# Decay sums of a linear-attention layer: one head behind each projection, and a stacked split matmul for their low-rank product

## The chip, the cores and the metric

The kernel runs on one core of a Trainium2 chip. The metric is the device time of one execution in microseconds. The kernel before took 2865.96 us, the median of three runs (2865.26 to 2868.37).

## The reference, cut to what matters

One inference step of a two-layer model: 128 context tokens and 1024 latent tokens, 1024 features. The first layer normalizes and modulates its input, projects it, and runs windowed attention beside a gated linear attention (GLA) with 4 heads in two directions. The change touches the projections and the decay of the GLA:

```python
h = rmsnorm(x, g) * (1 + scale) + shift
qa, ka, va, qb, kb, vb, rb, lr = split_cols(h @ w_in, SIZES_EVEN)   # lr: 2 directions x rank 16
...
la = log_sigmoid(einsum('btzr,zrk->btzk', lr, w_alpha) + b_alpha) / 16
la = la.reshape(B, T, 2, B_HEADS, B_DK)                             # 4 heads of 64, forward and backward
...
bcum = cumsum(la in chunks of 64 tokens)                            # the decay sums of the GLA
```

Keys and queries of the attention are rotated (`rope_2d`) behind their projection. The rest (attention, GLA, output projection, feed-forward, a recurrent second layer) is left as it is.

## The kernel before, in words

Features lie on the 128 partitions, the 1152 tokens (context first) on the free axis, in three column blocks of 384. A projection (`proj`, lines 292 to 302) is, for each column block, 8 times three matmuls: weights and activations are each split into a high and a low part of type fp32r, and `mm3` (lines 147 to 150) multiplies high by high, high by low, low by high. A weight tile comes through `wload` (lines 129 to 141): a transfer, ACT's cast to the high part (139), GpSimd's subtraction for the low part (140).

Memory is handed out in numbered slots of 128 x 1152: `us(i)` (line 84) is a new tile in slot i, and the first write into it waits until the tile that had the slot before has been read for the last time. `us(32)` and `us(33)` are halves of one pair (`up`, line 79). A matmul's target is a PSUM bank, 3 of the kind "mm", 2 of "S", 2 of "X", 1 of "O"; a bank is free when what it held has been read. The program is written as one sequence; a scheduler with a timeline simulation (line 1429) then fixes the order on each engine ahead of time, from its own costs. On the chip every engine and the transfer queue of SP work through their order strictly, so an instruction that waits holds up all behind it.

**The first stretch.** The input X lies in slots 16 to 23. Each column block is normalized in turn (`norm`, 281; `norm_k`, 263): sums of squares, row sums on TensorE (229), square root and reciprocal (231, 232), a broadcast on TensorE (239) copied by ACT (260), then for each of the 8 rows k a product on GpSimd (267), scale and shift on ACT or VectorE (272, 273, 275, 277) and the low part on VectorE (278). Nine blocks of 128 tokens are multiplied by the values', gates' and low-rank weights (lines 615 to 617), two tiles a block, 24 matmuls a tile. ACT copies the first tile of a block out (620), VectorE the second (620); line 623 copies the last 32 columns of the second, the low-rank factors `lr`, into `lrs3`. The norms of the second and third column block are started at block 2 and 5. Then TensorE transposes the low-rank columns (630) into `lrt` (631).

**The second stretch.** `gla_pre(hd)` (641 to 655) makes the decay sums of one head: for each column block a matmul of the 32 low-rank rows, fp32 (647), and a bias on ACT (648) into `et`; then on all 1152 tokens VectorE (649), Exp (650) and Ln (651) on ACT, each with a load of its table, VectorE (652), two scans of VectorE over 64 partitions, forward (653) and backward (654), into `bt`, and a store (655). `et` and `bt` have one slot each, 31 and 30, so a head's bias waits for the scans of the head before. The four heads stand in a row (657). Behind them come, in the program: the projection of the keys KA and its rotation (`rope`, 664 to 670: a shuffle, a product, GpSimd's product 669, a sum), the projection of the values VST and its transposes (705), the stacked split of the keys (`kstack`, 708 to 718), four query projections (720 to 724), each with its rotation and a store to `d_qa`; then the attention, which reads `d_qa` back (738, 744) and begins on TensorE at line 776. The scheduler spreads this over time; projections of the GLA's own keys and queries fill TensorE between. Line 192 is a piece of the modulation of later layers, spread over the kernel.

Of the kernel before, what the change touches and what calls it, by code (L numbers as in the profile page):

```python
# [8 lines left out]
F32R = mybir.dt.float32r  # L9
# [3 lines left out]
ALU = mybir.AluOpType  # L13
# [5 lines left out]
CW = 384  # L19
# [4 lines left out]
U = T  # L24
# [22 lines left out]
def body(tc, A):  # L47
    nc = tc.nc
    ve, sc, pe, gp, sy = nc.vector, nc.scalar, nc.tensor, nc.gpsimd, nc.sync

    def f_(ap):
        return ap.bitcast(F32)

    with contextlib.ExitStack() as ctx:
# [24 lines left out]
        def up(i, dt=F32):  # L79

            pair[i] = pu.tile([128, 2 * U], dt, tag=f"u{i}", name=f"u{i}", bufs=1)
            return pair[i]

        def us(i, dt=F32):

            if i in (0, 32):
                return up(i, dt)[:, :U]
            if i in (1, 33):
                return pair[i - 1][:, U:]
            return pu.tile([128, U], dt, tag=f"u{i}", name=f"u{i}", bufs=1)  # L90
# [7 lines left out]
        def mmps():  # L98
            if wide[0]:
                wide[0] = wide[0] % 8 + 1  # L100
                if wide[0] > 3 and wide[0] <= wide[1]:
                    return aux(*(("X", 2), ("X", 2), ("S", 2), ("S", 2), ("O", 1))[wide[0] - 4])
                if wide[0] > wide[1]:
                    wide[0] = 1
            return pm.tile([128, 512], F32, name="mm", bufs=3)

        def tmpa(n=CW):
            t = pt.tile([128, CW], F32, name="ta", bufs=3)
            return t[:, :n]

        def aux(tag="S", bufs=2):
            return pm.tile([128, 512], F32, name=tag, bufs=bufs)
# [8 lines left out]
        def wtile():  # L121

            if wext:
                wpos[0] = (wpos[0] + 1) % (4 + len(wext))
                if wpos[0] >= 4:
                    i = wext[wpos[0] - 4]
                    return uc(i - 100, F32R) if i >= 100 else us(i, F32R)[:, :D]
            return pw.tile([128, D], F32R, name="w", bufs=4)
# [3 lines left out]
        def wload(ap, n=D, slots=None, he=None):  # L132
            raw = pw.tile([128, D], F32, name="raw", bufs=3)
            sy.dma_start(out=raw[:, :n], in_=ap)
            if slots:
                hi, lo = us(slots[0], F32R), us(slots[1], F32R)
            else:
                hi, lo = wtile(), wtile()
            (he or wcopy[0])(hi[:, :n], raw[:, :n])  # L139
            gp.tensor_tensor(out=lo[:, :n], in0=raw[:, :n], in1=f_(hi[:, :n]), op=ALU.subtract)  # L140
            return hi, lo

        def split(hi, lo, src, e=None):
            sc.copy(hi, src)
            return (e or ve).tensor_tensor(out=lo, in0=src, in1=f_(hi), op=ALU.subtract)  # L145
# [13 lines left out]
        def ch(c):  # L159
            return slice(c * CW, (c + 1) * CW)  # L160
# [11 lines left out]
        def load_x(c):  # L172
            for k in range(8):
                sy.dma_start(out=X[k][:, ch(c)], in_=A["xT"][k, :, ch(c)])
# [117 lines left out]
        def projc(w, H, evict, c):  # L292
            hi, lo = w
            ps = mmps()
            for k in range(8):
                s = slice(k * 128, (k + 1) * 128)
                mm3(ps[:, :CW], hi[:, s], lo[:, s], H[0][k][:, ch(c)], H[1][k][:, ch(c)], k == 0, k == 7)
            evict(c, ps[:, :CW])

        def proj(w, H, evict):  # L300
            for c in range(NCH):
                projc(w, H, evict, c)
# [259 lines left out]
        d_qa = dr.tile([4, 128, T], F32, name="d_qa")  # L562
# [22 lines left out]
        H = [[None] * 8, [None] * 8]  # L585
# [15 lines left out]
                    sc.copy(wh[:, s], raw)  # L601
                    (gp if hf == 0 or i else ve).tensor_tensor(out=wl[:, s], in0=raw, in1=f_(wh[:, s]), op=ALU.subtract)
        load_x(2)
        lrs3 = us(32)[:, :288].rearrange("p (b n) -> p b n", b=9)
        for blk in range(9):
            if blk in (2, 5):
                norm(0, 0, X, H, 1 if blk == 2 else 2, inplace=True)
# [1 line left out]
            for hf in range(2):  # L609
                ps = mmps()  # L610
# [7 lines left out]
                n = 272 if hf == 0 else 240  # L618
# [3 lines left out]
                if hf == 1:  # L622
                    ve.tensor_copy(lrs3[:, blk], ps[:, 240:272])

        lrt = us(33)[0:32]
        for b0, b1 in ((0, 4), (4, 8), (8, 9)):
            ps = aux()
            n = (b1 - b0) * 128
            for b in range(b0, b1):
                pe.transpose(ps[0:32, (b - b0) * 128:(b - b0 + 1) * 128], lrs3[:, b], ident)  # L630
            ve.tensor_copy(lrt[:, b0 * 128:b1 * 128], ps[0:32, :n])

        RM = us(23)
        gp.memset(RM, 1.0)
        rm = RM.rearrange("p (c t) -> p c t", t=64)
        gp.memset(rm[0:64, :, 0:1], 0.0)
        gp.memset(rm[64:128, :, 63:64], 0.0)
        walp = us(22)[0:32, :512].rearrange("p (h n) -> p h n", h=4)
        sy.dma_start(out=walp, in_=A["w_alp"])

        def gla_pre(hd):

            et, bt = us(31), us(30)
            bal = cols[:, C_BALPHA + hd:C_BALPHA + hd + 1]
            for c in range(NCH):
                ps = aux()
                pe.matmul(ps[:, :CW], walp[:, hd], lrt[:, ch(c)], start=True, stop=True)
                sc.activation(out=et[:, ch(c)], in_=ps[:, :CW], func=AF.Identity, bias=bal)
            ve.scalar_tensor_tensor(bt, et, -1.0, et, op0=ALU.mult, op1=ALU.min)
            sc.activation(out=bt, in_=bt, func=AF.Exp)  # L650
            sc.activation(out=bt, in_=bt, func=AF.Ln, bias=1.0)
            ve.scalar_tensor_tensor(et, et, 0.0, bt, op0=ALU.min, op1=ALU.subtract)
            ve.tensor_tensor_scan(bt[0:64], RM[0:64], et[0:64], 0.0, op0=ALU.mult, op1=ALU.add)
            ve.tensor_tensor_scan(bt[64:128, ::-1], RM[64:128, ::-1], et[64:128, ::-1], 0.0, op0=ALU.mult, op1=ALU.add)
            sy.dma_start(out=d_b[hd], in_=bt)

        for hd in range(4):
            gla_pre(hd)

        COS, SIN = us(16), us(17)  # L660
        sy.dma_start(out=COS[:, :TL], in_=A["rope"][0])
# [2 lines left out]
        def rope(t):  # L664
            x = t[:, TC:T]
            r = us(19)[:, :TL]
            ve.stream_shuffle(r, x, [(i + 16) % 32 for i in range(32)])
            ve.tensor_tensor(out=x, in0=x, in1=COS[:, :TL], op=ALU.mult)
            gp.tensor_tensor(out=r, in0=r, in1=SIN[:, :TL], op=ALU.mult)
            ve.tensor_tensor(out=x, in0=x, in1=r, op=ALU.add)  # L670

        def ev_to(t):
            def ev(c, ps):
                sc.copy(t[:, ch(c)], ps)
            return ev

        KA, VST = us(18), us(20)
        proj(wload(A["w_ef"][4]), H, ev_to(KA))
        sy.dma_start(out=A["o_ck"], in_=KA[:, :TC])
        rope(KA)  # L680
        proj(wload(A["w_ef"][5]), H, ev_to(VST))
# [1 line left out]

        KK = [[us(24 + g * 2 + part, F32R) for part in range(2)] for g in range(2)]
        VA = [us(28, F32R), us(29, F32R)]
        SM = us(30, F32R)
        cst = tmpa(256)
        sy.dma_start(out=cst[:, 0:128], in_=A["cache_v"])
        sy.dma_start(out=cst[:, 128:256], in_=A["cache_k"])
        split(SM[:, 0:128], SM[:, 128:256], cst[:, 0:128])  # L690

        def va(part, blk):
            if blk == 9:
                return SM[:, part * 128:part * 128 + 128]
            return VA[part][:, blk * 128:(blk + 1) * 128]

        def kkc(g, part):
            o = 256 + (g * 2 + part) * 128
            return SM[:, o:o + 128]

        for b0, b1 in ((0, 4), (4, 8), (8, 9)):
            ps = aux()
            n = (b1 - b0) * 128
            for b in range(b0, b1):
                pe.transpose(ps[:, (b - b0) * 128:(b - b0 + 1) * 128], VST[:, b * 128:(b + 1) * 128], ident)
            split(VA[0][:, b0 * 128:b1 * 128], VA[1][:, b0 * 128:b1 * 128], ps[:, :n])

# [9 lines left out]
            kstack(cst[:, 128:256], KK[g][0][:, TL:U], KK[g][1][:, TL:U], g)  # L717
            kstack(KA[:, 0:TC], kkc(g, 0), kkc(g, 1), g)

        for j in range(4):  # L720
            q = us(21 + j % 2)
            proj(wload(A["w_ef"][j]), H, ev_to(q))
            rope(q)
            sy.dma_start(out=d_qa[j], in_=q)

# [530 lines left out]
        for blk in range(3):  # L1256
# [3 lines left out]
            g = gates_a(blk, 1)  # L1260
# [172 lines left out]
```

## Time and profile before

| | before |
|---|---|
| median of 3 runs | 2865.96 us (2865.26 to 2868.37) |
| profiled execution | 2866.14 us, span 2864.4 us |
| mean granted TensorE clock | 0.96 |
| TensorE busy | 2671.9 us, 93% |
| VectorE busy | 2036.7 us, 71% |
| ACT busy | 1333.5 us, 47% |
| GpSimd busy | 1280.0 us, 45% |
| chain that ended last | TensorE 73%, VectorE 12%, ACT 5%, transfers 5% |

PE is TensorE's matmul queue, DVE is VectorE, POOL is GpSimd, SP the queue of transfers. The span runs from the first to the last instruction; 1.7 us of the execution's own time lie around it. Busy time is the mean over a program of many stages, so a change in one stage is read in that stage's own rows.

### The profile page before, as it was taken

Reading aid. Unit: us, or ns where it says so; the run is one execution under the profiler, and the core shown is the slowest. Engines: PE = TensorE matmul, PEld = TensorE weight load, DVE = VectorE, ACT = ScalarE, POOL = GpSimd, SP = SyncE. Lnnn points to the kernel's source line nnn. Section 1 sums busy time; section 2 is a strip of 40 time slices with the busy share of each in tenths; the row PEclk is TensorE's granted clock in tenths of the full one; section 3 lists DMA queues with packets and bytes.
Section 4 is the critical chain, followed back from the end, with each engine's and each line's share of the span. In section 5 each row is a group of like instructions: output and inputs, shape, how many; then the busy total and the mean of one; then the engine's idle time right before and its main releaser. Section 6 shows DMA issues by size and latency. Waiting matters only on the chain.

```text
span 2864.4 us, 48327 instructions
## 1 busy us (share of the span) xinstructions
PE 2671.9 (93%) x18588; PEld 2540.8 (89%) x18588; DVE 2036.7 (71%) x3536; ACT 1333.5 (47%) x2402; POOL 1280.0 (45%) x767
## 2 busy tenths in 40 slices
PE   6999996888899999999999989896899999999998
PEld 4888884556899999999999989896899999999998
DVE  5466677653688877778786566657788777788876
ACT  5445556434543434444335567563543533444333
POOL 4231014223555556455556433333555555455453
PEclk8999997889999999999999999898999999999999
DMA  7125347643342233523223133373342233433322
GB/s 280 58 94 170 127 151 235 198 138 123 109 174 87 84 101 101 202 85 101 82 86 121 61 104 101 110 238 131 129 158 82 89 96 119 162 92 107 101 82 71
DMA packets 136966, 353.64 MB, mean 123 GB/s; under 512 B 14592, under 2 KB 61824, under 8 KB 136736
## 3 DMA queue, kind: packets, MB, share of 16 engines
q1 hardware_dynamic: 135008, 343.48, 36.3%
q0 software_dynamic: 1728, 7.08, 0.7%
q8 instruction: 146, 2.39, 0.3%
q14 instruction: 84, 0.69, 0.1%
HBM read 286.20 MB, written 64.30 MB: 122 GB/s over the span
## 4 chain that ended last, share of the span: by engine, by line
PE 73%; DVE 12%; ACT 5%; DMA 5%; issue 3%; POOL 1%; SPq 0%; DVEq 0%; ACTq 0%; POOLq 0%
PE mm L150 10%; PE mm L148 10%; PE mm L149 10%; PE X L150 5%; PE X L148 5%; PE X L149 5%; PE S L148 4%; PE S L150 4%; PE S L149 4%; PE O L148 2%; PE O L150 2%; PE O L149 2%; PE mm L192 1%; PE X L814 1%; DVE u L943 1%
## 5 line engine op out<-in xcount | busy, mean ns | idle before, releaser
L150 PE MATMUL mm<-u,w 128*128 128x384 f32 (+1 forms) x1320 | 420.9, 321 | 2.4 <-DVE w L458 2.0
L148 PE MATMUL mm<-u,w 128*128 128x288 f32 (+1 forms) x1234 | 396.6, 322 | 25.0 <-DVE u L317 23.1
L149 PE MATMUL mm<-u,w 128*128 128x288 f32 (+1 forms) x1234 | 393.4, 319 | 3.2 <-POOL u L145 3.2
L140 POOL TENSOR_TENSOR w<-raw,w 128x1024 fp32r<-128x1024 f32 (+1 forms) x66 | 150.3, 2278 | 361.3 <-ACT w L139 306.8
L148 PEld LDWEIGHTS mm<-u,w 128*128 128x128 f32 x1234 | 235.5, 191 | 33.8 <-issue 27.9
L150 PEld LDWEIGHTS mm<-u,w 128*128 128x128 f32 x1320 | 251.0, 190 | 7.5 <-issue 4.3
L149 PEld LDWEIGHTS mm<-u,w 128*128 128x128 f32 x1234 | 235.2, 191 | 4.6 <-POOL u L145 3.4
L150 PE MATMUL mm<-u,u 128*128 128x288 f32 x693 | 204.0, 296 | 0.0
L148 PE MATMUL S<-u,w 128*128 128x288 f32 (+1 forms) x526 | 164.9, 314 | 38.9 <-ACT t L1177 33.5
L317 DVE SCALAR_TENSOR_TENSOR u<-mm,mods,u 128x288 f32<-128x288 f32 (+4 forms) x345 | 145.8, 451 | 74.4 <-PE mm L150 73.7
L150 PE MATMUL X<-u,w 128*128 128x288 f32 (+1 forms) x630 | 192.8, 307 | 1.6 <-DVE w L450 1.6
L148 PE MATMUL mm<-u,u 128*128 128x288 f32 x627 | 186.5, 298 | 4.0 <-ACT u L444 3.8
L149 PE MATMUL mm<-u,u 128*128 128x288 f32 x627 | 185.3, 296 | 0.0
L148 PE MATMUL X<-u,w 128*128 128x288 f32 (+1 forms) x580 | 176.2, 306 | 1.4 <-DVE u L145 1.2
L149 PE MATMUL X<-u,w 128*128 128x288 f32 (+1 forms) x580 | 176.3, 305 | 1.1 <-DVE u L278 1.1
L149 PE MATMUL S<-u,w 128*128 128x288 f32 (+1 forms) x526 | 163.5, 311 | 0.0
L148 PE MATMUL mm<-u,c 128*128 128x288 f32 (+2 forms) x497 | 152.4, 307 | 0.7 <-DVE ta L505 0.7
L451 POOL TENSOR_TENSOR u<-raw 128x512 f32<-128x512 f32 x82 | 136.0, 1658 | 35.2 <-DMA raw<-in_w_fi_dram 19.4
L149 PE MATMUL mm<-u,c 128*128 128x288 f32 (+2 forms) x497 | 151.4, 305 | 0.0
L447 DVE TENSOR_TENSOR u<-u,raw 128x512 f32<-128x512 f32 x82 | 140.3, 1711 | 0.8
L148 PEld LDWEIGHTS S<-u,w 128*128 128x128 f32 x526 | 101.7, 193 | 41.8 <-ACT t L1177 35.6
L148 PE MATMUL X<-u,u 128*128 128x288 f32 (+1 forms) x444 | 131.9, 297 | 2.2 <-DVE u L145 1.5
(443 smaller groups left out, 9114.9 us busy)
## 6 DMA issues: line engine op xcount, KB each, us to landing
raw<-in_w_fi_dram SPq DMA_DIRECT2D x164, 512.0 KB, 3.6
raw<-in_w_fo_dram SPq DMA_DIRECT2D x96, 384.0 KB, 3.1
raw<-in_w_ada_dram SPq DMA_DIRECT2D x48, 512.0 KB, 4.9
c<-in_w_ada_dram SPq DMA_DIRECT2D x32, 512.0 KB, 5.9
d_w<-u SPq DMA_DIRECT2D x20, 512.0 KB, 4.0
u<-d_w SPq DMA_DIRECT2D x20, 512.0 KB, 4.8
u<-in_w_ada_dram SPq DMA_DIRECT2D x16, 512.0 KB, 10.3
raw<-in_w_fo_dram SPq DMA_DIRECT2D x16, 512.0 KB, 3.7
```

The costliest lines, as they stand in the source:

```text
L140: gp.tensor_tensor(out=lo[:, :n], in0=raw[:, :n], in1=f_(hi[:, :n]), op=ALU.subtract)
L148: pe.matmul(ps, wh, hh, start=first, stop=False)
L149: pe.matmul(ps, wh, hl, start=False, stop=False)
L150: pe.matmul(ps, wl, hh, start=False, stop=last)
L192: pe.matmul(ps[32 * g:32 * g + 32, :256], scp[:, 4 * p + g], raw[:, g * 256:(g + 1) * 256], start=p == 0, stop=p == 1)
L317: ve.scalar_tensor_tensor(x, ps[:, s0:s1], mod(l, j, cond, n), x, op0=ALU.mult, op1=ALU.add)
L447: ve.tensor_tensor(out=s2, in0=s1, in1=a11, op=ALU.subtract)
L451: gp.tensor_tensor(out=s3, in0=a11, in1=a21, op=ALU.subtract)
L814: pe.transpose(px[:, i * 128:(i + 1) * 128], P[i][:, kb * 128:(kb + 1) * 128], ident)
L943: ve.tensor_tensor_scan(kv[Bk, ::-1], D0[Bk, ::-1], kv[Bk, ::-1], 0.0, op0=ALU.mult, op1=ALU.add)
```

## The change

The decay sums of a head move: head 0 stands behind the projection of the keys, heads 1 and 2 behind the first two query projections, head 3 behind the third. The transposed low-rank factors and their weights are split into high and low parts and stacked on 96 partitions (high, high, low against high, low, high), so that one fp32r matmul of 96 rows takes the place of the fp32 one of 32 rows. The pair slot 32/33 now holds that stack, so `lrs3` moves to slot 21, which is X[5], and `w_alp` is loaded into slot 20, which is X[4].

```diff
@@ -601,7 +601,7 @@
                     sc.copy(wh[:, s], raw)
                     (gp if hf == 0 or i else ve).tensor_tensor(out=wl[:, s], in0=raw, in1=f_(wh[:, s]), op=ALU.subtract)
         load_x(2)
-        lrs3 = us(32)[:, :288].rearrange("p (b n) -> p b n", b=9)
+        lrs3 = us(21)[:, :288].rearrange("p (b n) -> p b n", b=9)
         for blk in range(9):
             if blk in (2, 5):
                 norm(0, 0, X, H, 1 if blk == 2 else 2, inplace=True)
@@ -622,21 +622,29 @@
                 if hf == 1:
                     ve.tensor_copy(lrs3[:, blk], ps[:, 240:272])
 
-        lrt = us(33)[0:32]
+        lw = up(32, F32R)
+        lrt = lw[:, :U]
         for b0, b1 in ((0, 4), (4, 8), (8, 9)):
             ps = aux()
             n = (b1 - b0) * 128
             for b in range(b0, b1):
                 pe.transpose(ps[0:32, (b - b0) * 128:(b - b0 + 1) * 128], lrs3[:, b], ident)
-            ve.tensor_copy(lrt[:, b0 * 128:b1 * 128], ps[0:32, :n])
+            g = slice(b0 * 128, b1 * 128)
+            for q in range(2):
+                sc.copy(lrt[q * 32:q * 32 + 32, g], ps[0:32, :n])
+            ve.tensor_tensor(out=lrt[64:96, g], in0=ps[0:32, :n], in1=f_(lrt[0:32, g]), op=ALU.subtract)
 
         RM = us(23)
         gp.memset(RM, 1.0)
         rm = RM.rearrange("p (c t) -> p c t", t=64)
         gp.memset(rm[0:64, :, 0:1], 0.0)
         gp.memset(rm[64:128, :, 63:64], 0.0)
-        walp = us(22)[0:32, :512].rearrange("p (h n) -> p h n", h=4)
-        sy.dma_start(out=walp, in_=A["w_alp"])
+        walp = lw[:, U:U + 512]
+        wa = us(20)[0:32, :512]
+        sy.dma_start(out=wa.rearrange("p (h n) -> p h n", h=4), in_=A["w_alp"])
+        for q in range(2):
+            sc.copy(walp[q * 64:q * 64 + 32], wa)
+        ve.tensor_tensor(out=walp[32:64], in0=wa, in1=f_(walp[0:32]), op=ALU.subtract)
 
         def gla_pre(hd):
 
@@ -644,7 +652,7 @@
             bal = cols[:, C_BALPHA + hd:C_BALPHA + hd + 1]
             for c in range(NCH):
                 ps = aux()
-                pe.matmul(ps[:, :CW], walp[:, hd], lrt[:, ch(c)], start=True, stop=True)
+                pe.matmul(ps[:, :CW], walp[0:96, hd * 128:hd * 128 + 128], lrt[0:96, ch(c)], start=True, stop=True)
                 sc.activation(out=et[:, ch(c)], in_=ps[:, :CW], func=AF.Identity, bias=bal)
             ve.scalar_tensor_tensor(bt, et, -1.0, et, op0=ALU.mult, op1=ALU.min)
             sc.activation(out=bt, in_=bt, func=AF.Exp)
@@ -654,9 +662,6 @@
             ve.tensor_tensor_scan(bt[64:128, ::-1], RM[64:128, ::-1], et[64:128, ::-1], 0.0, op0=ALU.mult, op1=ALU.add)
             sy.dma_start(out=d_b[hd], in_=bt)
 
-        for hd in range(4):
-            gla_pre(hd)
-
         COS, SIN = us(16), us(17)
         sy.dma_start(out=COS[:, :TL], in_=A["rope"][0])
         sy.dma_start(out=SIN[:, :TL], in_=A["rope"][1])
@@ -674,8 +679,10 @@
                 sc.copy(t[:, ch(c)], ps)
             return ev
 
-        KA, VST = us(18), us(20)
+        KA = us(18)
         proj(wload(A["w_ef"][4]), H, ev_to(KA))
+        gla_pre(0)
+        VST = us(20)
         sy.dma_start(out=A["o_ck"], in_=KA[:, :TC])
         rope(KA)
         proj(wload(A["w_ef"][5]), H, ev_to(VST))
@@ -683,6 +690,15 @@
 
         KK = [[us(24 + g * 2 + part, F32R) for part in range(2)] for g in range(2)]
         VA = [us(28, F32R), us(29, F32R)]
+        for j in range(2):
+            q = us(21 + j % 2)
+            proj(wload(A["w_ef"][j]), H, ev_to(q))
+            gla_pre(j + 1)
+            rope(q)
+            sy.dma_start(out=d_qa[j], in_=q)
+        q2 = us(21)
+        proj(wload(A["w_ef"][2]), H, ev_to(q2))
+        gla_pre(3)
         SM = us(30, F32R)
         cst = tmpa(256)
         sy.dma_start(out=cst[:, 0:128], in_=A["cache_v"])
@@ -717,9 +733,11 @@
             kstack(cst[:, 128:256], KK[g][0][:, TL:U], KK[g][1][:, TL:U], g)
             kstack(KA[:, 0:TC], kkc(g, 0), kkc(g, 1), g)
 
-        for j in range(4):
-            q = us(21 + j % 2)
-            proj(wload(A["w_ef"][j]), H, ev_to(q))
+        for j in range(2, 4):
+            q = q2
+            if j == 3:
+                q = us(22)
+                proj(wload(A["w_ef"][j]), H, ev_to(q))
             rope(q)
             sy.dma_start(out=d_qa[j], in_=q)
 
```

Three places of the order move what the prediction speaks of. First VectorE, behind the copies of line 623 of the first blocks. Before, each copy stands behind the copy of its own tile, beside the sums of squares (L252) of the third norm; `u32_427` is `lrs3`.

```order
L232 RECIPROCAL r_569<-r_569 128x3
L620 COPY ta_481<-mm_456 128x240
L623 COPY u32_427<-mm_456 128x32
L252 TENSOR_TENSOR t_788<-t_788,t_790 128x384
L252 TENSOR_TENSOR t_788<-t_788,t_793 128x384
L620 COPY ta_538<-mm_513 128x240
L623 COPY u32_427<-mm_513 128x32
L252 TENSOR_TENSOR t_788<-t_788,t_796 128x384
```

With the change, `lrs3` is `u21_427`, and the copies of blocks 0, 1 and 2 stand within the third norm, behind L273 of its row k=6 (`u22_98` is X[6]).

```order
L278 TENSOR_TENSOR u11_338<-S_839,u3_337 128x384
L273 TENSOR_SCALAR S_854<-u22_98,mods_73 128x384
L623 COPY u21_427<-mm_456 128x32
L623 COPY u21_427<-mm_513 128x32
L623 COPY u21_427<-mm_645 128x32
L278 TENSOR_TENSOR u14_363<-S_854,u6_362 128x384
L647 TENSOR_TENSOR u32_1091<-u20_1117,u32_1091 32x512
```

The copies moved from before the norm of the second column block to the middle of that of the third. Second, TensorE at the broadcast L239 of that third norm. Before, it stands between the tile `mm_759` (block 4) and `mm_863`.

```order
L616 MATMUL mm_759<-u30_385,u15_372 128x272
L617 MATMUL mm_759<-u31_386,u7_371 128x272
L239 MATMUL S_811<-ident_76,r_815 128x128 x3
L615 MATMUL mm_863<-u24_379,u0_312 128x272
L616 MATMUL mm_863<-u24_379,u8_313 128x272
L617 MATMUL mm_863<-u25_380,u0_312 128x272
```

With the change it stands between `mm_645` (the second tile of block 2) and `mm_674` (the first of block 3).

```order
L616 MATMUL mm_645<-u30_385,u15_372 128x272
L617 MATMUL mm_645<-u31_386,u7_371 128x272
L229 MATMUL S_811<-ones_75,t_788 128x1 x3
L239 MATMUL S_811<-ident_76,r_815 128x128 x3
L615 MATMUL mm_674<-u24_379,u0_312 128x272
L616 MATMUL mm_674<-u24_379,u8_313 128x272
```

So 12 of the 18 tiles, 288 matmuls, now stand behind this broadcast, where it was 8. `mm_674` takes the bank of `mm_456`, which L623 reads. Third, VectorE in the second stretch. Before, a rotation (L667, L668, L670) stands behind the first head, and the next heads follow with the key stack (L713) between.

```order
L649 SCALAR_TENSOR_TENSOR u30_1113<-u31_1112 128x1152
L652 SCALAR_TENSOR_TENSOR u31_1112<-u31_1112,u30_1113 128x1152
L653 SCALAR_TENSOR_TENSOR u30_1113<-u23_1106,u31_1112 64x1152
L654 SCALAR_TENSOR_TENSOR u30_1113<-u23_1106,u31_1112 64x1152
L667 STREAM_SHUFFLE u19_1275<-u18_1188 128x1024
L668 TENSOR_TENSOR u18_1188<-u18_1188,u16_1184 128x1024
L670 TENSOR_TENSOR u18_1188<-u18_1188,u19_1275 128x1024
L649 SCALAR_TENSOR_TENSOR u30_1131<-u31_1130 128x1152
L713 TENSOR_TENSOR u25_1366<-u18_1188,u24_1365 64x1024 x2
L713 TENSOR_TENSOR u27_1368<-u18_1188,u26_1367 64x1024 x2
```

With the change (L657 is what L649 was, L672 to L675 the rotation, L661 and L662 the scans), the rotation of the keys comes ahead of the first head, and a rotation stands behind the scans of every head.

```order
L672 STREAM_SHUFFLE u19_1231<-u18_1126 128x1024
L673 TENSOR_TENSOR u18_1126<-u18_1126,u16_1122 128x1024
L675 TENSOR_TENSOR u18_1126<-u18_1126,u19_1231 128x1024
L657 SCALAR_TENSOR_TENSOR u30_1212<-u31_1211 128x1152
L729 TENSOR_TENSOR u25_1322<-u18_1126,u24_1321 64x1024 x2
L729 TENSOR_TENSOR u27_1324<-u18_1126,u26_1323 64x1024 x2
L660 SCALAR_TENSOR_TENSOR u31_1211<-u31_1211,u30_1212 128x1152
L661 SCALAR_TENSOR_TENSOR u30_1212<-u23_1113,u31_1211 64x1152
L662 SCALAR_TENSOR_TENSOR u30_1212<-u23_1113,u31_1211 64x1152
L672 STREAM_SHUFFLE u19_1430<-u21_1327 128x1024
```

What moved is each rotation, ahead of its head's sums or between two heads. On TensorE the third product of each head stands among the projection's matmuls, after 100, 244, 326 and 401 matmuls of projections in this stretch; the first attention matmul comes behind 525 of them, where it was 504. The attention and all that follows keep their order: the last 14,561 instructions of TensorE are the same.

## Rows read from the trace of the kernel before

**Rows 1.** The page, busy time of the engine, share of the span, instructions

```profile
PE 2671.9 (93%) x18588; PEld 2540.8 (89%) x18588; DVE 2036.7 (71%) x3536; ACT 1333.5 (47%) x2402; POOL 1280.0 (45%) x767
```

**Rows 2.** Windows: us, PE, PEld, DVE, ACT, POOL busy, PE clock, DMA share, GB/s

```profile
150.00:175.00 25.00, 18.74 (x79) 15.46 (x80) 17.15 (x8) 8.32 (x10) 7.64 (x3) 0.80 0.20 67
```

**Rows 3.** Timeline of PE: start, us, engine, line, operation, count, [idle before <- releaser]

```profile
80.07 0.37 PE L615 MATMUL mm<-u,u 128*128 128x272 f32 x1
...
95.23 0.82 PE L630 MATMUL S<-ident,u 128*32 128x128 f32 x6
...
104.96 0.38 PE L630 MATMUL S<-ident,u 128*32 128x128 f32 x2
```

**Rows 4.** Timeline from 56 to 89 us, several engines

```profile
56.17 0.18 DVE L623 COPY u<-mm 128x32 f32<-128x32 f32 x1
...
71.06 1.02 DVE L278 TENSOR_TENSOR u<-S,u 128x384 fp32r<-128x384 f32 x2
...
76.54 0.26 ACT L231 ACTIVATE r<-S,epst 128x3 f32<-128x3 f32 x1
...
76.84 0.18 DVE L232 RECIPROCAL r<-r 128x3 f32<-128x3 f32 x1 [0.38 <-ACT r L231]
...
79.48 0.83 PE L239 MATMUL S<-ident,r 128*128 128x128 f32 x6
...
80.35 0.48 ACT L260 COPY t<-S 128x384 f32<-128x384 f32 x1 [3.55 <-PE S L239]
...
80.91 7.84 POOL L267 TENSOR_TENSOR u<-u,t 128x384 f32<-128x384 f32 x8 [11.97 <-ACT t L260]
...
87.98 0.68 DVE L273 TENSOR_SCALAR S<-u,mods 128x384 f32<-128x384 f32 x1
```

**Rows 5.** Windows of PE alone: us, PE busy, PE clock, DMA share, GB/s

```profile
160.00:162.00 2.00, 2.00 (x7) 0.50 0.00 0
162.00:164.00 2.00, 2.00 (x10) 0.76 0.00 0
164.00:166.00 2.00, 2.00 (x10) 1.00 0.01 4
```

**Rows 6.** Timeline of PE, second stretch

```profile
113.58 0.91 PE L647 MATMUL S<-u,u 32*128 32x384 f32 x2
...
156.26 1.65 PE L647 MATMUL S<-u,u 32*128 32x384 f32 x2 [6.70 <-ACT u L648]
...
182.80 0.27 PE L705 MATMUL S<-ident,u 128*128 128x128 f32 x1
...
218.24 1.07 PE L192 MATMUL mm<-raw,scp 128*32 128x256 f32 x16
...
222.43 0.41 PE L776 MATMUL S<-u,u 128*128 128x128 f32 x2 [2.25 <-DVE u L753]
```

**Rows 7.** Timeline of DVE, second stretch

```profile
122.48 1.36 DVE L652 SCALAR_TENSOR_TENSOR u<-u,u 128x1152 f32<-128x1152 f32 x1 [4.22 <-ACT u L651]
123.94 2.55 DVE L653 TENSOR_TENSOR_SCAN u<-u,u 64x1152 f32<-64x1152 f32 x1
126.52 4.58 DVE L654 TENSOR_TENSOR_SCAN u<-u,u 64x1152 f32<-64x1152 f32 x1
...
189.98 2.54 DVE L653 TENSOR_TENSOR_SCAN u<-u,u 64x1152 f32<-64x1152 f32 x1
192.53 2.56 DVE L654 TENSOR_TENSOR_SCAN u<-u,u 64x1152 f32<-64x1152 f32 x1
...
208.48 1.37 DVE L667 STREAM_SHUFFLE u<-u 128x1024 f32<-128x1024 f32 x1
...
213.90 1.23 DVE L670 TENSOR_TENSOR u<-u,u 128x1024 f32<-128x1024 f32 x1 [2.28 <-POOL u L669]
```

**Rows 8.** Timeline of POOL and ACT, second stretch

```profile
124.29 4.40 POOL L140 TENSOR_TENSOR w<-raw,w 128x1024 fp32r<-128x1024 f32 x1 [32.63 <-ACT w L139]
...
137.28 4.24 ACT L711 CAST u<-u 64x1024 fp32r<-64x1024 f32 x4 [3.98 <-DVE u L670]
```

## Prediction

> **What bounds the kernel now.** I first read the busy time of each engine: TensorE is busy for 93% of the span [rows 1], so as a rule time is lost only where it stands still or runs slow. Then I read the stretches of 25 us: from 150 to 175 us TensorE is busy for 18.7 of 25 us only, at a mean granted clock of 0.80, while VectorE is busy for 17.2 [rows 2]. That is where the decay sums of the four heads run. The order of both kernels shows that the change reorders only the start of the program, up to the attention: the last 14,561 instructions on TensorE are the same in the same order. So I work out two stretches, A up to the end of the low-rank tiles (104.96 us, the last transposes of line 630 [rows 3]) and B from there to the first attention matmul (222.43 us [rows 6]), and carry the sum to the end. It is made against the profiled execution of 2866.14 us; the median of the runs is 2865.96, so nothing is to be added for that. A measurement of this kernel can tell about 0.2%, 5.7 us, from no change.
>
> **Stretch A: the collected columns move into the slot of X[5].** Line 623 copies 32 low-rank columns out of each second tile, now 0.18 us right behind its tile [rows 4]. Its target was a free slot; it becomes `us(21)`, which is X[5] and is read until the norm of the third column block has done its row k=5. The order shows what follows: on VectorE the copies of blocks 0, 1 and 2 stand behind L273 of row k=6 of that norm, and until the first of them is done its PSUM bank is not free, so TensorE's seventh tile (mm_674) waits, and with it 12 tiles, 288 matmuls.
>
> When does that copy run? TensorE must first do L229 of the third norm, whose bank comes free with L278 of the second block, at 71.06 + 1.02 = 72.1 [rows 4]. Then L229 and its hand-over (1.4, an estimate, TensorE having just waited), L231 and L232 (76.54 to 77.02, so 0.5 [rows 4]), L239 (0.83 for six passes, 1.7 at half clock) and L260 (0.5): 76.2. In the kernel before, GpSimd's L267 starts at 80.91, just behind L260 [rows 4], because L239 stood behind whole tiles on TensorE. So the norm starts 4.65 us earlier. L273 of k=6 ended at 87.98 + 0.68 = 88.66; it ends at 84.0, and with the copy TensorE goes on at 84.3. It has waited since about 75.8, some 8.5 us. From there 288 matmuls at (95.23 - 80.07) / 120 = 0.1263 us [rows 3] take 36.4.
>
> After such a wait TensorE is slow: behind the idle 6.70 us in stretch B the products of line 647 take 1.65 instead of 0.91 us, and the granted clock is 0.50 from 160 to 162, 0.76 from 162 to 164 and 1.00 after that [rows 5, 6], so 1.2 GHz until about 163.0, 6.7 us from 156.26, half of it lost: 3.3 us. Stretch A ends at 84.3 + 36.4 + 3.3 = 124.0 instead of 104.96: **+19.0 us**.
>
> **Stretch B: one head behind each projection.** Before, it lasts 222.43 - 104.96 = 117.5 us. Counted from its start, VectorE's new order gives a chain:
> - The keys' projection: 72 matmuls at (218.24 - 182.80) / 203 = 0.1744 [rows 6] make 12.6, with the transposes 13.9; 1.6 for the last eviction and its hand-overs (an estimate). Then the rotation of the keys, which stands ahead of L657: 208.48 to 215.13, 6.65 [rows 7]: 22.1.
> - ACT runs the four copies of the key stack, 4.24 [rows 8], ahead of Exp: 26.4. Exp and Ln with their table loads: VectorE waits 4.22 for them in a row that overlaps part of the first load [rows 7]; with that part and an eviction 5.4 (an estimate): 31.8. L660 (1.36): 33.2.
> - The two scans: 2.55 + 4.58 beside a GpSimd subtraction of 4.40, or 2.54 + 2.56 without one [rows 7, 8]; 7.2 or 5.1. I take 7.2, since the subtraction of a weight load (line 140) now falls due beside every head, as each stands behind a projection of its own. First head done: 40.4.
> - A round for each further head, all on VectorE in this order: rotation 6.65, L657 1.36, waiting for Exp and Ln 4.22, L660 1.36, scans 7.16: 20.75. Three make 62.3, so the last scans end at 102.7. The rotation of the last query ends at 109.3.
> - From the end of that rotation to the first attention matmul it takes 222.43 - 215.13 = 7.3 [rows 6, 7]: **116.6**, so **-0.9 us**.
>
> TensorE does not set this end: it has 525 projection matmuls before the attention where it had 504 (91.6 us), 12 stacked products at 0.174 (2.1 us instead of 12 x 0.91 = 10.9 [rows 6]), about 4 us else. It waits at the third product of heads 2 and 3 (which waits for ACT's bias, for `et`, for the scans of the head before) and at the first attention matmul: about 2, 7 and 7 us. So what the stacked product saves is mostly waited away. The 21 matmuls done early come off later: 21 x 0.1744 = **-3.7**. The last wait leaves TensorE at 1.2 GHz behind the end of the stretch, which the kernel before did not pay after its 2.25 us there: **+3.3**.
>
> The added copies and subtractions of the split (eight copies on ACT, four subtractions on VectorE) I cost at nothing: they lie beside the low-rank tiles or in ACT's waits for TensorE; without that cover they are at most 12 times 1.05 (4.24 / 4, for tiles twice as wide [rows 8]), 12.6 us, about as far as the upper bound below. The load of `w_alp` now waits for the slot of X[4]; ACT's copy of it stands ahead of L277 of row k=5, but the tiles that read those rows come 18 us later. On SP's queue the stores of the decay sums now stand among the projections: behind that of the third head, which waits for its scans (about 82 us into B), stands the load of the eighth projection's weights, due at TensorE some 25 us later; its cast and subtraction take some 1 and 4.40 us [rows 8], which leaves 19 us for the transfer, so it is hidden; the stores behind the fourth head's are not waited for before the attention.
>
> **Sum**: 2866.1 + 19.0 - 0.9 - 3.7 + 3.3 = 2883.8, so **2884 us**. If all scans run alone, 4 x 2.1 = 8.2 comes off and with it the slow clock of the last wait, and the norm's chain may lose 1.4 less: 2871. If each scan is as long as the longest row, 4.58, the pairs cost 4 x 2.0 = 8.0 more, and the first wait of 2 us may cost a clock too (3.3): 2895.
>
> On the scans the Trainium skill ("SBUF — State Buffer", "Who interferes with whom") says that VectorE with two SBUF inputs and GpSimd share a port as an exclusive lock, held for a whole instruction. By that a pair pays one whole GpSimd operation at most. The rows agree in kind: the second scan and the subtraction are both near 4.5 us side by side. By that rule a pair is about 7.5 at most, the sum 1.4 us higher, and it speaks against spreading heads over the weight loads. Nothing above rests on it.
>
> **The rivals.**
> - *The decay chain is hidden* (0.07): rounds are so much shorter than 20.75 that TensorE never waits in B, as the scans ending sooner would allow. Then B is 91.6 + 2.1 + 4 = 97.7 us, 19.8 less, with the 3.7 makes -23.5: 2861.6. Against it: VectorE's own row of one round leaves 20.75, where a projection is 12.6.
> - *The seventh tile does not wait* (0.07): no loss in A, 2866.1 - 0.9 - 3.7 + 3.3 = 2865, no slower than before. It decides if L273 of k=6 were done when TensorE reaches that tile, about 75.8; the rows put it at 84.0, and the order is fixed, so little speaks for it. Both together (0.03): 2866.1 - 23.5 = 2843.
> - *Scans as long as the longest row*, GpSimd working through every one (0.13): 2892 to 2895. For it: five weight loads and four rotations on GpSimd in the same 117 us.
> - That the stacked product does not run in one pass: 12 x 0.91 instead of 2.1, 8.8 us of TensorE, most of it in waits that it has anyway; a few us, inside the range.
>
> **How the numbers follow.** The forecast has 0.70. The range reaches from 2864 (it takes in the tile that does not wait, and waits further on that swallow part of the delay) to 2895; outside it lie the hidden chain, both rivals together and a little of the long scans, some 0.13. Faster by over 5.7 us: 0.03 of both together and 0.02 of the tails of the two near 2862 and 2865: 0.05. Within: the other 0.12 of these. Slower: 0.83.
>
> **What would show it.** In the profile after: TensorE idle for 8 to 9 us around 76 to 84 us, released by VectorE's L623, with L623 three times in a row there; the low-rank transposes near 124 us; the scans about 20 us apart; waits of TensorE at the third stacked product behind ACT's L656; each product near 0.17 us; the first attention matmul near 240 us. I am wrong if L623 comes right behind its tiles, if the scans are under 15 us apart, or if the some 18 us by which the attention starts later are not found in the end.

## The result, and the profile after

The changed kernel took 2880.54 us, the median of 7 runs (2876.28 to 2890.70), beside 2865.96 us before (7 runs, 2860.52 to 2868.52): a ratio of 1.0062 with a 95% interval from 1.0047 to 1.0078, which is 17.8 us slower (13.5 to 22.4). The ratio takes in all the runs; the two medians by themselves lie 14.6 us apart. The forecast was 2884 us, 17.7 us slower than the profiled execution before. The profiled execution of the changed kernel took 2879.78 us, its span 2878.0 us, 13.6 us more than before. The page's busy times show no loss: TensorE works as long as it did [rows 1], over a longer span.

```profile
span 2878.0 us, 48329 instructions
...
PE 2670.6 (93%) x18576; PEld 2546.9 (88%) x18576; DVE 2022.2 (70%) x3537; ACT 1337.8 (46%) x2409; POOL 1284.8 (45%) x767
```

**Stretch A.** The timeline of TensorE around the third norm (start, us, engine, line, operation, count, [idle before <- releaser]):

```profile
65.31 0.39 PE L615 MATMUL mm<-u,u 128*128 128x272 f32 x1 [2.78 <-ACT ta L620]
...
73.00 1.44 PE L229 MATMUL S<-ones,t 128*128 128x1 f32 x6 [2.88 <-DVE u L278]
...
75.00 1.65 PE L239 MATMUL S<-ident,r 128*128 128x128 f32 x6 [0.56 <-DVE r L232]
...
84.95 0.56 PE L615 MATMUL mm<-u,u 128*128 128x272 f32 x1 [8.30 <-DVE u L623]
...
123.53 1.04 PE L631 MATMUL S<-ident,u 128*32 128x128 f32 x8
```

Four waits stand in a row, and the long one, 8.30 us, is ended by line 623, the copies of the low-rank columns. From 59 us to the transposes TensorE stands for 14.5 us in all, where it stood 1.1, and it is busy for 50.0 us instead of 44.9, at a mean granted clock of 0.84 instead of 1.00. VectorE's timeline shows why they come so late, three in one row of 0.37 us behind L273:

```profile
84.04 0.68 DVE L273 TENSOR_SCALAR S<-u,mods 128x384 f32<-128x384 f32 x1
84.63 0.37 DVE L623 COPY u<-mm 128x32 f32<-128x32 f32 x3
```

And the windows of TensorE (us, busy, granted clock, DMA share, GB/s) show the clock at 1.2 GHz (0.50) during the wait and for about 4.9 us after it:

```profile
83.00:85.00 2.00, 0.05 (x1) 0.50 0.39 152
...
87.00:89.00 2.00, 2.00 (x11) 0.50 0.00 0
89.00:91.00 2.00, 2.00 (x15) 0.79 0.00 0
91.00:93.00 2.00, 2.00 (x18) 1.00 0.19 70
```

The transposes behind the last tile start at 123.53 us, where it was 104.96 [rows 3]: 18.6 us later.

**Stretch B.** TensorE's products, the modulation's matmuls before which it waits last, and the first attention matmul (line 794):

```profile
162.57 0.51 PE L655 MATMUL S<-u 96*128 96x384 f32 x2
...
185.44 0.69 PE L655 MATMUL S<-u 96*128 96x384 f32 x1 [2.71 <-ACT u L656]
...
205.15 0.45 PE L655 MATMUL S<-u 96*128 96x384 f32 x1 [4.31 <-ACT u L656]
...
232.55 1.93 PE L192 MATMUL mm<-c,scp 128*32 128x256 f32 x16 [5.45 <-DVE t L862]
...
239.44 0.34 PE L794 MATMUL S<-u,u 128*128 128x128 f32 x2
```

Two products now take 0.51 us together where two recorded passes of one took 0.91 [rows 6], and yet TensorE stands for 12.5 us in this stretch, where it stood 10.7: from 123.53 to 239.44 it lasts 115.9 us instead of 117.5. VectorE's scans give the pace (the first scan of each head):

```profile
156.36 4.64 DVE L661 TENSOR_TENSOR_SCAN u<-u,u 64x1152 f32<-64x1152 f32 x1
161.01 2.55 DVE L662 TENSOR_TENSOR_SCAN u<-u,u 64x1152 f32<-64x1152 f32 x1
...
177.52 4.62 DVE L661 TENSOR_TENSOR_SCAN u<-u,u 64x1152 f32<-64x1152 f32 x1
...
197.22 4.63 DVE L661 TENSOR_TENSOR_SCAN u<-u,u 64x1152 f32<-64x1152 f32 x1
...
217.39 4.41 DVE L661 TENSOR_TENSOR_SCAN u<-u,u 64x1152 f32<-64x1152 f32 x1
```

They are 21.2, 19.7 and 20.2 us apart. The first attention matmul stands 17.0 us later than before [rows 6].

**Behind it**, one correction of the part ahead of the prediction: the last 14,561 instructions of TensorE do keep their order, but they begin only at about 700 us, so the attention and the decayed attention are in another order as well, which was not priced. The view of one tile (bank O: first and last start in us) gives a mark behind them; first before, then after:

```profile
L149 PE MATMUL O<-u,w x212: 290/295/522, 803.5 to 2823.0; 128*128 128x288 f32 x78, 128*128 128x384 f32 x28
```

```profile
L149 PE MATMUL O<-u,w x212: 290/295/522, 823.1 to 2836.6; 128*128 128x288 f32 x78, 128*128 128x384 f32 x28
```

There the delay is 19.6 us. From that mark to the end the span before has 2060.9 us left, after 2054.9, with the same instructions in the same order, so this part differs by 6.0 us between two executions without a change in it. The eight experiments below have 2052.8 to 2060.5 us left there; in their traces only one, weights_on_vector, keeps this order (2056.1), and the others have it changed in places. What moves this part is not shown. The whole is therefore read from the many timed runs, and the stretches from the marks.

### The profile page after: what moved, and what is told of

Same layout as the page of the kernel before. It is cut to its first block, busy times and chain, and to the rows that moved or that the text cites. A ratio compares the mean times of both kernels' runs of the same rounds, so it can differ in the third digit from the quotient of the medians.

```text
span 2878.0 us, 48329 instructions
## 1 busy us (share of the span) xinstructions
PE 2670.6 (93%) x18576; PEld 2546.9 (88%) x18576; DVE 2022.2 (70%) x3537; ACT 1337.8 (46%) x2409; POOL 1284.8 (45%) x767
## 4 chain that ended last, share of the span: by engine, by line
PE 72%; DVE 11%; ACT 6%; DMA 5%; issue 4%; POOL 1%; SPq 0%; DVEq 0%; ACTq 0%; POOLq 0%
PE mm L150 10%; PE mm L148 10%; PE mm L149 10%; PE X L150 5%; PE X L148 5%; PE X L149 5%; PE S L148 4%; PE S L150 4%; PE S L149 4%; PE O L148 2%; PE O L149 2%; PE O L150 2%; PE mm L192 1%; PE X L832 1%; DMA raw<-in_w_fi_dram 1%
```

## The experiments

The theory at this point: stretch A costs the whole loss, by the slot alone; stretch B is paced by VectorE's chain of rotation, sums and scans, so that neither the faster product nor the new order of heads moves it much. The rival: the new order costs the time. Stretch A is measured to the transposes behind the last tile, B from there to the first attention matmul. Each was timed beside the kernel before on the same chip; the ratio is to that.

**free_slot** gives the low-rank columns of blocks 0 to 7 a place that nothing else uses; block 8 alone stays in X[5]'s slot. Its edit to the changed kernel, cut to where the columns lie:

```diff
-        lrs3 = us(21)[:, :288].rearrange("p (b n) -> p b n", b=9)
+        lrs8 = st.tile([128, 256], F32, name="lrs8").rearrange("p (b n) -> p b n", b=8)
+        lrs = [lrs8[:, b] for b in range(8)] + [us(21)[:, :32]]
```

> The changed kernel with the low-rank columns of blocks 0 to 7 in a tile of their own (block 8 alone goes to X[5]'s slot), nothing else. Theory (the slot holds TensorE's seventh tile): no wait on VectorE's low-rank copies, the low-rank transposes at about 105 us as before, the second stretch as in the changed kernel, 115.9 us, so the first attention matmul at about 221 us; total 2861 to 2866, ratio to before 0.998 to 1.000. Rival (the heads spread over the projections cost the time): the second stretch is longer than 117.5 us and the total stays above 2875.

2860.87 us, ratio 0.9982 (0.9971 to 0.9993): the loss is gone, and by the timed runs the rest of the change is a small gain. That gain is not found in the two stretches: the transposes stand 2.1 us later than before, not at about 105 us as expected, and the first attention matmul 0.6 us later. TensorE's timeline:

```profile
107.06 0.38 PE L632 MATMUL S<-ident,lrs 128*32 128x128 f32 x2
...
168.29 0.44 PE L656 MATMUL S<-u 96*128 96x384 f32 x1 [2.71 <-ACT u L657]
...
187.98 0.69 PE L656 MATMUL S<-u 96*128 96x384 f32 x1 [4.30 <-ACT u L657]
...
222.98 0.34 PE L795 MATMUL S<-u,u 128*128 128x128 f32 x2
```

B is 115.9 us, to the tenth that of the changed kernel, with the same waits of 2.71 and 4.30 us at the third products. The rival is out: with the stacked product, the order of heads costs nothing that these runs can tell.

**slot_alone** does only the opposite to the kernel before:

```diff
-        lrs3 = us(32)[:, :288].rearrange("p (b n) -> p b n", b=9)
+        up(32)
+        lrs3 = us(21)[:, :288].rearrange("p (b n) -> p b n", b=9)
```

> The kernel before with the low-rank columns put into X[5]'s slot, nothing else: four heads in a row, fp32 product. Theory: TensorE waits about 8 us for VectorE's low-rank copies near 76 to 85 us, the transposes come at about 123.5 us, and the total is 18 to 20 us above before, 2883 to 2887, ratio 1.006 to 1.007. Rival: within 3 us of before. If the wide spread of the changed kernel's times (2876 to 2891) comes from the waits at a low clock in the first stretch, it shows here too.

2881.68 us, ratio 1.0056 (1.0043 to 1.0068), 16 us slower and just under the 18 to 20 that were expected.

```profile
83.75 0.57 PE L616 MATMUL mm<-u,u 128*128 128x272 f32 x1 [8.31 <-DVE u L624]
...
122.31 1.04 PE L631 MATMUL S<-ident,u 128*32 128x128 f32 x8
...
240.59 0.41 PE L777 MATMUL S<-u,u 128*128 128x128 f32 x2 [2.47 <-DVE u L754]
```

One line of the change brings the wait of 8.31 us and all of the loss. On the spread: its times lie 9 us apart, those of the kernel before, over 27 runs, 13 us (2858.61 to 2871.44), so slot_alone shows no wider spread. Whether the changed kernel's 14 us have a cause of their own stays open.

**product_alone** and **order_alone** split what is left. The first is the kernel before with the stacked product and the low-rank columns in a tile of their own, four heads in a row; the second moves the heads only (its edit, cut to the first moves):

```diff
-        for hd in range(4):
-            gla_pre(hd)
...
         proj(wload(A["w_ef"][4]), H, ev_to(KA))
+        gla_pre(0)
...
+            proj(wload(A["w_ef"][j]), H, ev_to(q))
+            gla_pre(j + 1)
```

> The kernel before with the stacked split product and the low-rank columns in a tile of their own, the four heads still in a row. Theory (TensorE waits for the scans, so the 8.8 us that the product saves are waited away): the second stretch 114 to 118 us, total 2862 to 2867. Rival (the product's passes count in full): 8 to 9 us less, 2857.

> The kernel before with the heads moved behind the projections as in the change, but with the fp32 product and the low-rank columns where they were. In its order TensorE has all six products of heads 2 and 3 behind the 288th matmul of the projections. Theory (TensorE stands at a head's third product until the scans of the head before are done): TensorE stands there for 20 us or more, the second stretch is 122 to 128 us, total 2869 to 2876. Rival (the place of the products does not matter, since VectorE's chain sets the end anyway): second stretch 114 to 118 us, total 2860 to 2866.

product_alone: 2863.35 us, ratio 0.9984 (0.9972 to 0.9995), B 115.1 us:

```profile
105.03 0.38 PE L632 MATMUL S<-ident,lrs 128*32 128x128 f32 x2
...
220.17 0.66 PE L785 MATMUL S<-u,u 128*128 128x128 f32 x2 [5.67 <-DVE u L762]
```

order_alone: 2868.11 us, ratio 1.0012 (1.0001 to 1.0022), just under the expected 2869; B 122.5 us, with two waits that make 16.2 us, where 20 or more were expected:

```profile
105.76 0.38 PE L630 MATMUL S<-ident,u 128*32 128x128 f32 x2
...
168.70 4.20 PE L647 MATMUL S<-u,u 32*128 32x384 f32 x6 [5.47 <-ACT u L648]
183.60 1.64 PE L647 MATMUL S<-u,u 32*128 32x384 f32 x2 [10.70 <-ACT u L648]
...
228.23 0.41 PE L786 MATMUL S<-u,u 128*128 128x128 f32 x2 [1.11 <-DVE u L763]
```

So B is 117.5 before, 115.1 with the product, 122.5 with the order, 115.9 with both. Within B the product gives 2.4 of the 8.8 us that TensorE saves; the new order adds nothing to it, and by itself costs 5.0, since the scheduler then lets TensorE come to the last head's product before the scans ahead of it are done. Neither difference is left at the mark in bank O, which stands at 803.5 us before, at 803.7 with the product and at 802.5 with the order: the stretch between, in another order each time, takes 581.1, 583.5 and 574.3 us. The slot's delay is still there, 824.8 us in slot_alone.

**two_buffers** asks whether the single slots of `et` and `bt` pace the heads. The split values, which have slots 28 and 29 otherwise, get them behind the last head:

```diff
-            et, bt = us(31), us(30)
+            et, bt = (us(31), us(30)) if hd % 2 == 0 else (us(29), us(28))
```

> As free_slot, and every other head has its own two slots for its bias output and its sums (28 and 29, the split values get them behind the last head), so a head's product and bias don't wait for the scans of the head before. Theory (VectorE's chain of rotation, sums and scans sets the end of the stretch, not the slots): TensorE no longer waits at the third products, the scans still end about 20 us apart, the first attention matmul moves by less than 3 us against free_slot, total within 4 us of it. Rival (the slots are what chains the heads): the scans under 17 us apart and 10 us or more off the total.

2858.33 us, ratio 0.9970 (0.9962 to 0.9979). The third product of head 2 no longer waits and that of head 3, against the expectation, still waits 2.66 us (4.30 in free_slot):

```profile
180.56 0.44 PE L656 MATMUL S<-u 96*128 96x384 f32 x1 [2.66 <-ACT u L657]
...
222.28 0.34 PE L795 MATMUL S<-u,u 128*128 128x128 f32 x2
```

But VectorE keeps its pace: the first scans of the heads start at 140.23, 161.39, 180.14 and 201.48 us, the attention at 222.28 (free_slot: 222.98), and B is 114.2 us, 1.7 less. TensorE waits elsewhere, 7.13 and 4.66 us at the transposes of the values. The slots set little of it; the chain is VectorE's, as the theory has it.

**rope_on_vector** and **weights_on_vector** shorten links of that chain, each in free_slot:

```diff
-            gp.tensor_tensor(out=r, in0=r, in1=SIN[:, :TL], op=ALU.mult)
+            ve.tensor_tensor(out=r, in0=r, in1=SIN[:, :TL], op=ALU.mult)
```

```diff
-        proj(wload(A["w_ef"][5]), H, ev_to(VST))
+        proj(wload(A["w_ef"][5], le=ve), H, ev_to(VST))
```

(`le` is the engine of the low part's subtraction; the four query projections likewise.)

> As free_slot, and the rotation's product with the sines is on VectorE (1.2 us) instead of GpSimd (3.4 us, for which VectorE waits 2.3). Theory (VectorE's chain sets the end of the second stretch, and rotations are links of it): each rotation is 1.0 to 1.5 us shorter, the first attention matmul 5 to 7 us earlier than in free_slot, total 2853 to 2857. Rival (TensorE or ACT sets that end): under 2 us, since VectorE then has more work.

> As free_slot, and the low parts of the weights of the values' and the four query projections are subtracted on VectorE instead of GpSimd. Theory (a scan waits until GpSimd's subtraction has ended): all scans beside these loads take 2.5 to 2.6 us instead of 4.6, 2.1 us less a head, while each subtraction adds 1.2 to 1.4 us to VectorE: 2 to 4 us off the second stretch, total 2856 to 2860. Rival (the first scan of a pair is slow by itself): scans stay at 4.6 us and the stretch gets 5 us longer.

rope_on_vector: 2858.69 us, ratio 0.9981 (0.9967 to 0.9995), B 112.5 us, 3.4 less than in free_slot, and the attention at 218.39 us, 4.6 earlier and not 5 to 7: the rotations are 1.1 us shorter as expected, but the second head's scan still starts 21.1 us behind the first's (136.94 and 158.04), as its rotation waits 1.66 us for a copy of TensorE's projection (L680). weights_on_vector: 2862.77 us, ratio 0.9986 (0.9975 to 0.9998), B 112.4 us, 3.5 less. Both totals lie above what was expected, and by the timed runs neither is told from free_slot; by B both are shorter. VectorE's scans in weights_on_vector, without and with a subtraction left on GpSimd:

```profile
134.35 2.55 DVE L662 TENSOR_TENSOR_SCAN u<-u,u 64x1152 f32<-64x1152 f32 x1
136.91 2.55 DVE L663 TENSOR_TENSOR_SCAN u<-u,u 64x1152 f32<-64x1152 f32 x1
...
176.65 4.62 DVE L662 TENSOR_TENSOR_SCAN u<-u,u 64x1152 f32<-64x1152 f32 x1
```

```profile
176.24 2.62 POOL L140 TENSOR_TENSOR w<-raw,w 128x1024 fp32r<-128x1024 f32 x1 [6.28 <-ACT w L139]
```

The rival said that the first scan of a pair is slow by itself. It is not: 4.62 us where GpSimd works (176.24 to 178.86), 2.55 where it doesn't.

**all_three** is two_buffers with both moves to VectorE:

> two_buffers with the rotation's product and these subtractions on VectorE. Theory: the savings add, the scans end 16 to 18 us apart, first attention matmul 8 to 13 us earlier than in free_slot (222.98 us), total 2847 to 2853. Rival (VectorE's added work eats them): within 3 us of two_buffers, 2856 to 2861.

2849.98 us (2848.70 to 2851.41), ratio 0.9947 (0.9935 to 0.9959): B 108.5 us, the attention 9.2 us earlier than in free_slot.

```profile
105.20 0.38 PE L632 MATMUL S<-ident,lrs 128*32 128x128 f32 x2
...
213.74 0.34 PE L795 MATMUL S<-u,u 128*128 128x128 f32 x2
```

The scans start 24.8, 16.8 and 18.3 us apart. The first of these gaps, which missed the expected 16 to 18, is set by the projection: VectorE stands 3.55 us for ACT's cast, which itself waited 3.51 us for the projection's matmuls. It is faster than the kernel before by 15 us and, by the two ratios, than the changed one by some 33 us, though it was not timed beside that.

## Why the prediction was right

- **The wait in A: right, and by its own steps.** TensorE to go on at 84.3 us after 8.5 us of waiting; it did at 84.95 after 8.30. The broadcast's copy was to end at 76.2 us and L273 of row k=6 at 84.0; they ended at 77.2 and 84.7. End of A forecast at 124.0, measured 123.53; +19.0 forecast, +18.6 measured. slot_alone shows the cause by itself and free_slot its absence.
- **The clock behind it:** 3.3 us forecast, from a half-speed run of 6.7 us. Here it was 1.2 GHz from 84.95 to about 89.8, which costs half of that, 2.4. A little smaller, and in part made up for by the later start.
- **The chain in B: right in mechanism, a little long.** First scans to end 40.4 us into B, measured 163.56 - 123.53 = 40.0; rounds of 20.75, measured 21.2, 19.7, 20.2; first attention matmul 116.6, measured 115.9. In the two later rounds the rotation took 6.1 instead of 6.65, as no subtraction stood before it on GpSimd.
- **TensorE's waits** were put at about 2, 7 and 7 us: they were 2.71, 4.31 and 5.45, 12.5 in all instead of 16, and the last stood before the modulation's matmuls, not before the attention. The stacked product ran in one pass, at 0.17 us each; product_alone gives its worth within B, 2.4 us of 8.8. The copies of the split, costed at nothing, end at 130.4 us, before VectorE stands 8.11 us for the projection, so they cost nothing there.
- **The last two terms were not right.** The 3.3 us for a clock still at 1.2 GHz behind the stretch: the windows of TensorE show it low inside the stretch and at full speed where the attention begins at 239.44, so its cost is already in the 115.9.

```profile
232.00:234.00 2.00, 1.45 (x16) 0.50 0.94 369
234.00:236.00 2.00, 2.00 (x13) 0.50 0.31 89
236.00:238.00 2.00, 2.00 (x12) 0.85 1.06 286
238.00:240.00 2.00, 2.00 (x16) 1.00 1.01 392
```

  And the 3.7 us of 21 matmuls done early are not found: from the first attention matmul to the mark in bank O it takes 583.7 us, 581.1 before, 579.8 in free_slot. There the order is another in each of these three kernels, against what the prediction said of it ("reorders only the start of the program, up to the attention"). The two terms nearly cancelled, +3.3 and -3.7 against a measured +2.6 for that stretch. What the attention's order itself is worth stays open; it was not tried alone.
- **The sum** of +17.7 is met by the timed runs, 17.8 (13.5 to 22.4). That it is met to a tenth is chance: the two profiled executions lie 13.6 us apart, +18.6 in A, -1.6 in B, +2.6 up to the mark and -6.0 behind it, and the last two are not explained.
- **The rivals.** The tile that does not wait (2865 us) is what free_slot shows on purpose, at 2860.87. The hidden chain did not occur in any run; all_three, with B at 108.5, still stands 11 us above the 97.7 that TensorE alone would need. Scans all as long as the longest row did not occur: each pair had one long scan.

## What to carry to other kernels

When a buffer moves into a slot that something else still reads, look not at the moved write, which was 0.18 us here, but at what the waiting write holds: it held a PSUM bank, the bank held TensorE's next tile, and the tile held 288 matmuls behind it. Before a product is made cheaper, ask whose wait it lies in: 8.8 us saved on TensorE gave 2.4 in its stretch, while two moves that gave VectorE more work, off a slower engine that it waited for, helped to take 7.4 us off the stretch. And an order of instructions that a scheduler makes must be compared to its end, not to the place where one thinks the change ends.

## What the runs showed of the hardware

A scan and GpSimd's subtraction don't share time, they take turns. In the changed kernel the subtraction is first, and the scan that begins 0.4 us later ends 2.4 us after it, one scan's own time (2.55):

```profile
155.96 2.64 POOL L140 TENSOR_TENSOR w<-raw,w 128x1024 fp32r<-128x1024 f32 x1 [11.93 <-ACT w L139]
```

In rope_on_vector the scan is first, from 158.04 for 2.55 us to 160.59; the subtraction, issued at 158.73, ends 2.2 us after that scan; and the next scan, issued at 160.60, then ends 2.4 us after the subtraction:

```profile
158.73 4.06 POOL L140 TENSOR_TENSOR w<-raw,w 128x1024 fp32r<-128x1024 f32 x1 [10.91 <-ACT w L139]
```

```profile
158.04 2.55 DVE L662 TENSOR_TENSOR_SCAN u<-u,u 64x1152 f32<-64x1152 f32 x1
160.60 4.60 DVE L663 TENSOR_TENSOR_SCAN u<-u,u 64x1152 f32<-64x1152 f32 x1
```

The Trainium skill ("SBUF — State Buffer", "Who interferes with whom") says that a VectorE instruction with two SBUF inputs contends with a GpSimd instruction that reads SBUF, that the ports they share are an exclusive lock, and that the order of issue decides who blocks. The runs agree, and show it for scans of 64 partitions, at 1.9 to 2.1 us a head in the changed kernel (4.41 to 4.64 us against 2.55), and that the way out is cheap: a subtraction of the same size took 1.22 us on VectorE.
